# Recurrent stage in a written order: VectorE and ScalarE as listed, one conversion moved to GpSimd, weights earlier

## The chip, the cores and the metric

The kernel runs on one core of one Trainium2 chip. The metric is the device time of the whole kernel in microseconds, as the median of several runs. One execution was also recorded by the hardware profiler; its own time stands beside its trace. Engines: PE (TensorE, matrix products), DVE (VectorE), ACT (ScalarE), POOL (GpSimd), SP (SyncE, which issues most DMAs).

## The reference, cut to what matters

Two decoder layers on 1024 positions of width 1024 in fp32. Layer 0 is causal attention with 12 heads (low-rank queries and keys, rotary parts); layer 1 is a gated linear recurrence. Both layers also attend with 4 heads to 256 memory tokens, multiply by a SiLU gate, project out and normalise.

```python
def causal_attention(q, k, v):                      # layer 0, 12 heads
    sc = einsum('bqhd,bkhd->bhqk', q_blk, k) * scale
    p = softmax(where(mask, sc, -inf))
    return einsum('bhqk,bkhd->bqhd', p, v)

def rg_lru_branch(u, ...):                          # layer 1
    xc = conv_b + sum(u_pad[:, t:t + s] * conv_w[t] for t in range(4))
    xb = xc.reshape(b, s, 12, 64)
    r = sigmoid(einsum('bsgi,gij->bsgj', xb, w_r) + b_r)
    i = sigmoid(einsum('bsgi,gij->bsgj', xb, w_i) + b_i)
    log_a = (-8 * softplus(-lam)) * r
    a = exp(log_a)
    gated_x = sqrt(-expm1(2 * log_a)) * (i * xc)
    return scan(h = a * h + gated_x)

for layer in range(2):
    z = h @ w_in                                    # mixer inputs | gate | q_mem
    tok = causal_attention(...) if layer == 0 else rg_lru_branch(...)
    mem_out = memory_attention(q_mem, mem_k, mem_v)
    y = concat([tok, mem_out]) * silu(gate)
    h = layer_norm(ALPHA * h + y @ w_out)
```

## The kernel before

**Split numbers.** A product of two fp32 matrices is made of three products on PE with operands split into a high part (rounded to the format PE reads fast) and a low part (the rest). `split` (lines 88 to 90) makes both: the high part by the engine named, always the low part by DVE (line 90). `load_w` (line 98) loads a block of weights of 128 x 1024 into one of two staging tiles `wf` by a DMA on SP's queue and splits it into the next pair of a ring of tiles, with the high part by GpSimd in this stage (line 82).

**The recurrent stage** (lines 939 to 1082) works on six tiles t of 128 channels by 1024 positions. For each tile:

- u: 48 products of 512 columns (`proj_T`, lines 113 to 115) project the layer's input by the weights `w1[t]` into a pair of PSUM banks. u0 and u1 come first, while layer 0's last norm blocks still finish; their weights are in tiles `st`, those of later ones in R16/R17 or rg0/rg1 by turns.
- c (`lru_copy`): ACT copies the two banks to U.
- v (`lru_conv`): DVE makes the convolution, one two-operand step (line 1006) and three three-operand ones (line 1009) in place in XC, which read U and XC, both in SBUF. XC is then split into XH and XL; XH is made by ACT here.
- r (`lru_rest`): 12 gate products of XH and XL on PE into two pairs of banks, four sigmoids on ACT into RR and II; then on ACT an exponential (a), a hyperbolic tangent, the square of a (written over XC, line 1027) and a square root (line 1029), and on DVE the product II*XC (line 1026), a combination of XC and RR (line 1028), the product RR*II (line 1030) and the scan (line 1031).

U, XC, XH, XL, RR and II have two buffers, chosen by t mod 2. After the six tiles follow two projections for the memory queries (q0, q1; `qmem_proj`) and gate blocks 6 and 7 (g).

**Who sets the order.** Each engine runs its own instructions strictly in order. The program is written in the order of the string `ORD`, and a scheduler of the build rearranges all engines by its own estimates; a section under `tc.manual_schedule(engines=...)` keeps the named engines in the order in which the program is written. Before, no engine was kept in this stage. What each engine then has is quoted in the section on the change.

**Two other places.** In layer 0, `max_pass` finds each query's largest score for a coming head while the current heads are worked on. `neg_max_row` then waits `DELAY` units of work (3; a unit is one block of scores) and has PE transpose the maxima (line 433); DVE copies them (line 435), and a DMA puts them into a row of the query tile. After each pair of heads, `finish_pair` (line 624) sends the denominators through memory and multiplies the pair by their reciprocals on GpSimd (line 634). Slots 0 to 5 are the pairs of layer 0's heads, 6 and 7 the memory heads of layer 0, 8 and 9 those of layer 1. In `attn_unit` the low part of the softmax weights (`pl`, in layer 1 `mpl`, line 564) comes from DVE or GpSimd, and PE's products wait for it.

Of the kernel before, what the change touches and what calls it, by code (L numbers as in the profile page):

```python
# [15 lines left out]
ALU = mybir.AluOpType  # L16
# [4 lines left out]
S = 1024  # L21
# [23 lines left out]
def hybrid_kernel(ctx: ExitStack, tc: tile.TileContext, io):  # L45
    nc = tc.nc
    PE, ACT, DVE, POOL, SP = nc.tensor, nc.scalar, nc.vector, nc.gpsimd, nc.sync
# [6 lines left out]
    def open_pool(name, side="left"):  # L54
        p = tc.tile_pool(name=name, bufs=1, reuse_waits="tile", side=side)
        return p, p.__enter__()
# [8 lines left out]
    R16 = main.tile([128, S], F32R, name="R16")  # L65
    R17 = main.tile([128, S], F32R, name="R17")
# [21 lines left out]
    def split(src, hi, lo, eng):  # L88
        hi_copy(eng, hi, src)
        DVE.tensor_tensor(out=lo, in0=src, in1=f32(hi), op=ALU.subtract)  # L90

    wjob = [0]
    ring = {"hi": [R[10], R16], "lo": [R[11], R17]}
# [6 lines left out]
    def load_w(ap, n):  # L100
        j = wjob[0]
        wjob[0] += 1
        st = wf[j % 2][:, :n]
        SP.dma_start(st, ap)
        nb = len(ring["hi"])
        hi, lo = ring["hi"][j % nb], ring["lo"][j % nb]
        wsplit(st, hi[:, :n], lo[:, :n])
        return hi, lo
# [143 lines left out]

    HALF = [slice(0, 512), slice(512, 1024)]

    def qmem_proj(layer, m, ap, mh, ml, thi, tlo, ps):
        hi, lo = load_w(ap, S)
        proj_T(ps, hi, lo, mh, ml, 8)
        for n, cs in enumerate(HALF):
            ACT.copy(thi[n], ps[n])
            DVE.tensor_tensor(out=tlo[n], in0=ps[n], in1=f32(thi[n]), op=ALU.subtract)  # L260
            SP.dma_start(qmem_d[layer][m, 0][:, cs], f32(thi[n]))
            SP.dma_start(qmem_d[layer][m, 1][:, cs], f32(tlo[n]))

    for m in range(2):
        qmem_proj(0, m, io["w0"][8 + m], lambda n: [x[:, HALF[n]] for x in xh], lambda n: [x[:, HALF[n]] for x in xl],
                  ph[2 * m:2 * m + 2], pl[2 * m:2 * m + 2], next_ps())


# [109 lines left out]
    def run_all(g):  # L378
        for _ in g:
            pass  # L380
# [43 lines left out]
                rows.remove(r)  # L424
                r[1]()

    def neg_max_row(mx, dst_row):
        nm = small.tile([128, 8], F32, tag="nm", name="nm")
        DVE.tensor_reduce(out=nm, in_=mx, axis=AX.X, op=ALU.max, negate=True)

        def row():
            ps = next_m()
            PE.transpose(ps[0:8, 0:128], nm, ident)
            nmt = small.tile([8, 128], F32R, tag="nmt", name="nmt", bufs=1)
            DVE.tensor_copy(nmt, ps[0:8, 0:128])
            SP.dma_start(f32(dst_row()).rearrange("o (a b) -> o a b", a=8), f32(nmt))
        rows.append([DELAY, row])

    def max_pass(h, halves=None):
        kh_, kl_, qh_, ql_ = sets[h % 4] if not halves else [None] * 4  # L440
        mx = small.tile([128, 8, 2], F32, tag="mx", name="mx")
        POOL.memset(mx, -3.0e38)
        for i in range(8):
            n = (i + 1) * 128
            step = 320 if n == 640 and not halves else 512
            for a in range(0, n, step):
                w = min(step, n - a)
                j = min(a, 512) // step
                out = next_m()[:, 0:w]
                if halves:  # L450
                    q, k = halves[2 + i // 4][0:96, i % 4 * 128:(i % 4 + 1) * 128], halves[a // 512][0:96, 0:w]
                else:
                    q, k = qh_[0:96, i * 128:(i + 1) * 128], kh_[0:96, a:a + w]
                PE.matmul(out, q, k, start=True, stop=True)  # L454
                if a + w == (i + 1) * 128:
                    DVE.tensor_tensor_reduce(out=out, in0=out, in1=cmask[:, 512 - w:512], scale=1.0, scalar=-3.0e38,  # L456
                                             op0=ALU.add, op1=ALU.max, accum_out=mx[:, i, j:j + 1])
                else:
                    DVE.tensor_reduce(out=mx[:, i, j:j + 1], in_=out, axis=AX.X, op=ALU.max)
                yield  # L460
        neg_max_row(mx, lambda: sets[h % 4][2][96:97, :])
        yield

    sets = [[p0[1].tile([128, S], F32R, tag=f"g{j}", name=f"st0_{j}") for j in range(4)]]
# [159 lines left out]
    def finish_pair(gt, slot):  # L624
        rn = small.tile([128, 16], F32, tag="rn", name="rn")
        for e in range(2):
            SP.dma_start(rn[:, e * 8:(e + 1) * 8], den[32 * e:32 * e + 1, :].rearrange("o (a b) -> o a b", a=128))
        DVE.reciprocal(rn, rn)
        for e in range(2):
            SP.dma_start(den_d[slot, e].rearrange("(a b) -> a b", a=128), rn[:, e * 8:(e + 1) * 8])  # L630
        rec = Of[slot % 2]
        for e in range(2):
            SP.dma_start(rec[e * 64:(e + 1) * 64, :], den_d[slot, e:e + 1, :].broadcast_to([64, S]))
        POOL.tensor_tensor(out=gt, in0=gt, in1=rec, op=ALU.mult)

    SC = 1.0 / math.sqrt(96.0)

# [305 lines left out]

    weng[0] = POOL
    wjob[0] = 0
    ring["hi"], ring["lo"] = [sets[i][2] for i in (1, 2, 3)], [sets[i][3] for i in (1, 2, 3)]
    u_ps = []
    for t in range(2):
        hi, lo = load_w(io["w1"][t], S)
        ps = pair(t)  # L950
        proj_T(ps, hi, lo, hth, htl, 8)
        u_ps.append(ps)
# [3 lines left out]
    G1 = GA + [pc0[1].tile([128, S], F32, name=f"GB{i}") for i in range(4)]  # L956
    rg = [pc0[1].tile([128, S], F32R, name=f"rg{i}") for i in range(2)]
    ring["hi"], ring["lo"] = [R16, rg[0]], [R17, rg[1]]
    pc = open_pool("pc")
    U = [pc[1].tile([128, S + 3], F32, name=f"U{i}") for i in range(2)]  # L960
    XC = [pc[1].tile([128, S], F32, name=f"XC{i}") for i in range(2)]
# [37 lines left out]
    def lru_copy(t, ps):  # L999
        for n in range(2):  # L1000
            ACT.copy(U[t % 2][:, 3 + n * 512:3 + (n + 1) * 512], ps[n])

    def lru_conv(t):
        b = t % 2
        up, xc = U[b], XC[b]
        DVE.tensor_scalar(out=xc, in0=up[:, 0:S], scalar1=vecs[:, CW + 4 * t:CW + 4 * t + 1],
                          scalar2=vecs[:, CB + t:CB + t + 1], op0=ALU.mult, op1=ALU.add)
        for j in range(1, 4):
            DVE.scalar_tensor_tensor(out=xc, in0=up[:, j:j + S], scalar=vecs[:, CW + 4 * t + j:CW + 4 * t + j + 1],
                                     in1=xc, op0=ALU.mult, op1=ALU.add)  # L1010
        split(xc, XH[b], XL[b], ACT)

    def lru_rest(t):
        b = t % 2
        xc, rr, ii = XC[b], RR[b], II[b]
        for w, (dst, bias) in enumerate(((rr, BR), (ii, BI))):
            ps = pair(3 * (1 - w))
            o = t * 256 + w * 128
            proj_T(ps, WGH[:, o:o + 128], WGL[:, o:o + 128], lambda n: [XH[b][:, HALF[n]]],
                   lambda n: [XL[b][:, HALF[n]]], 1)  # L1020
            for n, cs in enumerate(HALF):
                ACT.activation(dst[:, cs], ps[n], AF.Sigmoid, bias=vecs[:, bias + t:bias + t + 1])
        a = G1[t]
        ACT.activation(a, rr, AF.Exp, scale=cf[:, t:t + 1])
        ACT.activation(rr, rr, AF.Tanh, scale=cf[:, t:t + 1])
        DVE.tensor_tensor(out=ii, in0=ii, in1=xc, op=ALU.mult)
        ACT.activation(xc, a, AF.Square)
        DVE.scalar_tensor_tensor(out=rr, in0=xc, scalar=1.0, in1=rr, op0=ALU.add, op1=ALU.mult)
        ACT.activation(rr, rr, AF.Sqrt, scale=-1.0)
        DVE.tensor_tensor(out=ii, in0=rr, in1=ii, op=ALU.mult)  # L1030
        DVE.tensor_tensor_scan(out=G1[t], data0=a, data1=ii, initial=0.0, op0=ALU.mult, op1=ALU.add)
# [3 lines left out]
    def next_p():  # L1035
        psj[0] += 1
        return pair(1 + (psj[0] - 1) % 2)

    def lru_u(t):
        hi, lo = load_w(io["w1"][t], S)  # L1040
        ps = next_p()
        proj_T(ps, hi, lo, hth, htl, 8)
        u_ps.append(ps)

    gw = {}
    gorder = [6, 7, 0, 1, 2, 3, 4, 5]

    def gate_load(m):
        gw[m] = load_w(io["w1"][6 + m], S)
# [13 lines left out]
                DVE.tensor_tensor(out=G1[m][:, cs], in0=ps[n], in1=G1[m][:, cs], op=ALU.mult)  # L1063
            yield

    ORD = 'c0 v0 c1 v1 r0 u2 c2 v2 r1 u3 c3 v3 r2 u4 c4 v4 r3 u5 c5 v5 r4 q0 r5 q1 g6 g7'
    for it in ORD.split():
        t = int(it[1])
        if it[0] == 'c':
            lru_copy(t, u_ps[t])  # L1070
        elif it[0] == 'v':
            lru_conv(t)
        elif it[0] == 'r':
            lru_rest(t)
        elif it[0] == 'u':
            lru_u(t)
        elif it[0] == 'g':
            gate_load(t)
            run_all(gate1(t, next_p()))
        else:  # L1080
            qmem_proj(1, t, io["w1"][14 + t], hth, htl, [QH[:, c] for c in HALF], [QL[:, c] for c in HALF], next_p())
    close_pool(pc)

    pd = open_pool("pd")
# [120 lines left out]
```

## Time and profile before

| | |
|---|---|
| median of 3 runs | 928.58 us (928.46 to 929.18) |
| the profiled execution | 926.91 us, of which the span from first to last instruction is 925.1 us |
| PE busy | 896.5 us (97%) |
| DVE, ACT, POOL busy | 594.9, 442.5, 223.6 us |
| mean granted clock of PE | 0.994 of full speed |

Idle time counts where it is PE's, since PE is busy nearly all the time. A timeline row gives the start and the duration in us, the engine, the source line, the operation, what it writes and reads, and in brackets how long the engine stood idle before it and what ended that. Matrix products are pipelined: one of 512 columns is shown with 0.39 us, but the next starts some 0.233 us later.

### The profile page before, as it was taken

How to read it: one execution, taken by the hardware profiler on the slowest of the kernel's cores; microseconds unless marked ns; L12 is line 12 of the kernel's file. 1: busy time of each engine (PE TensorE's matmuls, PEld its weight loads, DVE VectorE, ACT ScalarE, POOL GpSimd, SP SyncE). 2: the span in 40 equal slices, each digit the busy share in tenths (PEclk: the TensorE clock that was granted, in tenths of full speed). 3: DMA queues.
4: the chain of work that ended last, by engine and by line, in shares of the span. 5: the costliest groups of instructions: out<-in, count | busy, mean ns of one | idle time of the engine just before them, and what ended most of it. 6: DMA issues, size and time to landing. Idle time of an engine off the chain costs nothing.

```text
span 925.1 us, 12456 instructions
## 1 busy us (share of the span) xinstructions
PE 896.5 (97%) x4477; PEld 734.5 (79%) x4477; DVE 594.9 (64%) x1207; ACT 442.5 (48%) x764; POOL 223.6 (24%) x219
## 2 busy tenths in 40 slices
PE   9999999999999999999999999988999999999996
PEld 8998888877787778779676888866888877678886
DVE  7953346258877768796785597636997154457655
ACT  4422311217676677776785222117997156753000
POOL 5100023111526364473682100000000032210000
PEclk9999999999999999999999999998999999999999
DMA  8102133314022213055647653111112911252411
GB/s 309 63 16 108 55 102 127 125 63 116 17 61 69 59 58 105 15 150 159 202 117 239 203 191 102 53 69 46 45 46 109 242 50 47 69 183 91 153 75 46
DMA packets 45945, 96.08 MB, mean 104 GB/s; under 512 B 10906, under 2 KB 20282, under 8 KB 45884
## 3 DMA queue, kind: packets, MB, share of 16 engines
q1 hardware_dynamic: 45308, 94.47, 32.7%
q8 instruction: 35, 0.57, 0.3%
q10 hardware_dynamic: 576, 0.82, 0.3%
q14 instruction: 26, 0.21, 0.1%
HBM read 71.94 MB, written 23.16 MB: 103 GB/s over the span
## 4 chain that ended last, share of the span: by engine, by line
PE 81%; DVE 7%; ACT 6%; issue 3%; DMA 2%; POOL 1%; SPq 0%; DVEq 0%; ACTq 0%; POOLq 0%
PE bank L113 10%; PE bank L114 10%; PE bank L115 10%; PE bank L846 6%; PE bank L847 6%; PE bank L848 6%; PE bank L572 6%; PE bank L657 5%; PE bank L367 3%; PE bank L369 3%; PE bank L368 3%; PE bank L154 2%; PE bank L155 2%; PE bank L153 2%; PE bank L454 2%
## 5 line engine op out<-in xcount | busy, mean ns | idle before, releaser
L564 POOL TENSOR_TENSOR pl<-Pf,ph 128x512 fp32r<-128x512 f32 (+1 forms) x99 | 125.5, 1277 | 115.5 <-ACT ph L562 102.4
L561 ACT ACTIVATE Pf<-bank 128x512 f32<-128x512 f32 (+1 forms) x152 | 86.4, 569 | 50.2 <-DVE bank L558 20.0
L657 PE MATMUL bank<-st,st 96*128 96x512 f32 (+7 forms) x432 | 105.4, 343 | 0.1
L90 DVE TENSOR_TENSOR R<-wf,R 128x1024 fp32r<-128x1024 f32 (+4 forms) x43 | 52.6, 1226 | 63.9 <-POOL R L82 59.9
L657 PEld LDWEIGHTS bank<-st,st 96*128 96x128 f32 (+1 forms) x432 | 75.5, 189 | 13.3 <-ACT ph L562 0.6
L562 ACT ACTIVATE ph<-bank 128x512 fp32r<-128x512 f32 (+1 forms) x136 | 76.3, 562 | 0.1
L82 POOL TENSOR_SCALAR R<-wf 128x1024 fp32r<-128x1024 f32 (+3 forms) x25 | 24.1, 966 | 199.3 <-PE bank L114 96.1
L113 PE MATMUL bank<-R,R 128*128 128x256 f32 (+1 forms) x190 | 63.2, 333 | 0.7 <-ACT Pf L375 0.4
L114 PE MATMUL bank<-R,R 128*128 128x256 f32 (+1 forms) x190 | 62.3, 328 | 0.0
L115 PE MATMUL bank<-R,R 128*128 128x256 f32 (+1 forms) x190 | 62.2, 327 | 0.0
L456 DVE CUSTOM_DVE_ANT_0 bank<-bank,cmask 128x384 f32<-128x384 f32 (+4 forms) x96 | 48.8, 518 | 9.8 <-PE bank L454 9.0
L367 PE MATMUL bank<-xh,R 128*128 128x512 f32 x128 | 50.9, 398 | 0.1
L369 PE MATMUL bank<-xh,R 128*128 128x512 f32 x128 | 50.7, 396 | 0.0
L368 PE MATMUL bank<-xl,R 128*128 128x512 f32 x128 | 50.5, 395 | 0.0
L572 PE MATMUL bank<-ph,VH 128*65 128x512 f32 (+2 forms) x144 | 49.3, 342 | 0.0
L123 ACT ACTIVATE rq_t<-lnv 128x1 f32<-128x1 f32 x16 | 3.3, 203 | 94.3 <-DVE lnv L897 94.3
L572 PE MATMUL bank<-pl,VH 128*65 128x512 f32 (+2 forms) x144 | 44.9, 339 | 2.3 <-POOL pl L564 1.9
L892 DVE SCALAR_TENSOR_TENSOR GA<-GA,bank 128x512 f32<-128x512 f32 (+1 forms) x34 | 22.0, 648 | 38.9 <-PE bank L848 38.6
L572 PE MATMUL bank<-ph,VL 128*65 128x512 f32 (+2 forms) x144 | 46.8, 337 | 0.0
L847 PE MATMUL bank<-wo,yh 128*128 128x512 f32 (+1 forms) x126 | 46.8, 372 | 0.0
L846 PE MATMUL bank<-wo,yh 128*128 128x512 f32 (+1 forms) x126 | 46.7, 370 | 0.0
L848 PE MATMUL bank<-wo,yl 128*128 128x512 f32 (+1 forms) x126 | 45.9, 368 | 0.0
(313 smaller groups left out, 2444.0 us busy)
## 6 DMA issues: line engine op xcount, KB each, us to landing
wf<-w SPq DMA_DIRECT2D x26, 512.0 KB, 3.5
wf<-wout SPq DMA_DIRECT2D x16, 512.0 KB, 4.2
Of<-den_d SPq DMA_DIRECT2D x20, 256.0 KB, 3.6
GA<-x SPq DMA_DIRECT2D x8, 512.0 KB, 3.9
h_d<-GA SPq DMA_DIRECT2D x8, 512.0 KB, 2.6
GA<-h_d SPq DMA_DIRECT2D x8, 512.0 KB, 4.0
y_d<-GA SPq DMA_DIRECT2D x7, 512.0 KB
out<-GA SPq DMA_DIRECT2D x7, 512.0 KB
```

Of the source, the lines that this page charges most:

```text
L113: PE.matmul(out, lh, rh, start=(i == 0), stop=False)
L114: PE.matmul(out, lh, rl, start=False, stop=False)
L115: PE.matmul(out, ll, rh, start=False, stop=(i == n - 1))
L367: PE.matmul(ps[n], hi[:, ks], xh[k][:, cs], start=(k == 0), stop=False)
L369: PE.matmul(ps[n], lo[:, ks], xh[k][:, cs], start=False, stop=(k == 7))
L561: ACT.activation(pf[:, :n], ps[:, :n], AF.Exp, scale=scale)
L564: lo_eng.tensor_tensor(out=lo[:, :n], in0=pf[:, :n], in1=f32(hi)[:, :n], op=ALU.subtract)
L572: mm.append(lambda: PE.matmul(ops[0:65, q0:q0 + w], st, mv[:, c0:c0 + w], start=start, stop=stop))
L657: yield lambda: PE.matmul(ps[:, c0:c0 + w], k[0:r, ks], q[0:r, qs], start=(i == 0), stop=(i == 2))
L846: PE.matmul(out, hi, woh[k][:, ns], start=(k == ko[0]), stop=False)
L847: PE.matmul(out, hi, wol[k][:, ns], start=False, stop=False)
L848: PE.matmul(out, lo, woh[k][:, ns], start=False, stop=(k == ko[7]))
```

## The change

Six things, all in the order of work or in who does it:

- In the recurrent stage DVE and ACT are kept in the written order, and `ORD` is written anew. `lru_rest` is cut in two: `lru_gates` (letter r) keeps the gate products and the sigmoids, and `lru_rest` (letter b) the remaining ACT and DVE work. The next tile's convolution (v) is listed behind the gates and ahead of the next b.
- XH is made by GpSimd, not by ACT.
- The weights are loaded two steps ahead (letters l, k, h), where before each load came with its use. Those of u2 and u3 are asked for before the projections of u0 and u1 are made, ahead of the gate matrices `wg` on SP's queue.
- u0 and u1 keep their weights in the `st` tiles 1 and 3, where they were in 1 and 2.
- `qmem_proj` takes weights that are loaded already.
- For even heads the maxima are transposed 5 units later, where it was 3.
- The product in `finish_pair` is made by DVE for slots 7, 8 and 9.

```diff
-    def qmem_proj(layer, m, ap, mh, ml, thi, tlo, ps):
-        hi, lo = load_w(ap, S)
+    def qmem_proj(layer, m, w, mh, ml, thi, tlo, ps):
+        hi, lo = w
...
-    def neg_max_row(mx, dst_row):
+    def neg_max_row(mx, dst_row, delay=DELAY):
...
-        rows.append([DELAY, row])
+        rows.append([delay, row])
...
-        neg_max_row(mx, lambda: sets[h % 4][2][96:97, :])
+        neg_max_row(mx, lambda: sets[h % 4][2][96:97, :], 5 if h % 2 == 0 else DELAY)
...
-        POOL.tensor_tensor(out=gt, in0=gt, in1=rec, op=ALU.mult)
+        eng = DVE if slot >= 7 else POOL
+        eng.tensor_tensor(out=gt, in0=gt, in1=rec, op=ALU.mult)
...
-    ring["hi"], ring["lo"] = [sets[i][2] for i in (1, 2, 3)], [sets[i][3] for i in (1, 2, 3)]
+    ring["hi"], ring["lo"] = [sets[i][2] for i in (1, 3)], [sets[i][3] for i in (1, 3)]
     u_ps = []
+    uw = [load_w(io["w1"][t], S) for t in range(2)]
+    ring["hi"], ring["lo"] = [R16], [R17]
+    gw = {2: load_w(io["w1"][2], S)}
     for t in range(2):
-        hi, lo = load_w(io["w1"][t], S)
+        hi, lo = uw[t]
...
     ring["hi"], ring["lo"] = [R16, rg[0]], [R17, rg[1]]
+    gw[3] = load_w(io["w1"][3], S)
...
-        split(xc, XH[b], XL[b], ACT)
-
-    def lru_rest(t):
+        split(xc, XH[b], XL[b], POOL)
+
+    def lru_gates(t):
         b = t % 2
         xc, rr, ii = XC[b], RR[b], II[b]
         for w, (dst, bias) in enumerate(((rr, BR), (ii, BI))):
...
                 ACT.activation(dst[:, cs], ps[n], AF.Sigmoid, bias=vecs[:, bias + t:bias + t + 1])
+
+    def lru_rest(t):
+        b = t % 2
+        xc, rr, ii = XC[b], RR[b], II[b]
         a = G1[t]
...
     def lru_u(t):
-        hi, lo = load_w(io["w1"][t], S)
+        hi, lo = gw[t]
...
-    ORD = 'c0 v0 c1 v1 r0 u2 c2 v2 r1 u3 c3 v3 r2 u4 c4 v4 r3 u5 c5 v5 r4 q0 r5 q1 g6 g7'
+    ORD = ('c0 v0 c1 r0 u2 v1 b0 c2 v2 l4 r1 u3 b1 c3 v3 l5 r2 u4 b2 c4 v4 k0 r3 u5 b3 c5 v5 k1 '
+           'r4 b4 q0 h6 r5 b5 q1 h7 g6 g7')
+    with tc.manual_schedule(engines={mybir.EngineType.DVE, mybir.EngineType.Activation}):
+        for it in ORD.split():
...
+            elif it[0] == 'b':
+                lru_rest(t)
+            elif it[0] == 'l':
+                gw[t] = load_w(io["w1"][t], S)
+            elif it[0] == 'k':
+                gw[t + 20] = load_w(io["w1"][14 + t], S)
...
+            elif it[0] == 'h':
+                gate_load(t)
```

VectorE at the start of the stage, where tiles 0 and 1 are convolved: what stood there before.

```order
L1006 TENSOR_SCALAR XC0_5392<-U0_5390,vecs_69 128x1024
L1006 TENSOR_SCALAR XC1_5393<-U1_5391,vecs_69 128x1024
L1009 SCALAR_TENSOR_TENSOR XC0_5392<-U0_5390,vecs_69,XC0_5392 128x1024
L1009 SCALAR_TENSOR_TENSOR XC1_5393<-U1_5391,vecs_69,XC1_5393 128x1024
L1009 SCALAR_TENSOR_TENSOR XC0_5392<-U0_5390,vecs_69,XC0_5392 128x1024
```

And what stands there now (WGL is the low part of the gate matrices):

```order
L1011 TENSOR_SCALAR XC0_5398<-U0_5396,vecs_69 128x1024
L1014 SCALAR_TENSOR_TENSOR XC0_5398<-U0_5396,vecs_69,XC0_5398 128x1024 x2
L90 TENSOR_TENSOR WGL_5411<-wf1_83,WGH_5410 128x768
L1014 SCALAR_TENSOR_TENSOR XC0_5398<-U0_5396,vecs_69,XC0_5398 128x1024
L90 TENSOR_TENSOR XL0_5402<-XC0_5398,XH0_5400 128x1024
L1011 TENSOR_SCALAR XC1_5399<-U1_5397,vecs_69 128x1024
```

Tile 0's convolution and split are now complete before tile 1's first step; before, the two tiles took turns.

VectorE in the loop, from the recurrence of tile 0 to that of tile 1, before (R17 is the low part of a weight block, GA0 the scan's result):

```order
L1026 TENSOR_TENSOR II0_5400<-II0_5400,XC0_5392 128x1024
L1028 SCALAR_TENSOR_TENSOR RR0_5398<-XC0_5392,RR0_5398 128x1024
L1030 TENSOR_TENSOR II0_5400<-RR0_5398,II0_5400 128x1024
L1006 TENSOR_SCALAR XC0_5392<-U0_5390,vecs_69 128x1024
L1031 SCALAR_TENSOR_TENSOR GA0_72<-GA0_72,II0_5400 128x1024
L1009 SCALAR_TENSOR_TENSOR XC0_5392<-U0_5390,vecs_69,XC0_5392 128x1024
L1026 TENSOR_TENSOR II1_5401<-II1_5401,XC1_5393 128x1024
L1009 SCALAR_TENSOR_TENSOR XC0_5392<-U0_5390,vecs_69,XC0_5392 128x1024
L90 TENSOR_TENSOR R17_71<-wf0_82,R16_70 128x1024
L1009 SCALAR_TENSOR_TENSOR XC0_5392<-U0_5390,vecs_69,XC0_5392 128x1024
L1028 SCALAR_TENSOR_TENSOR RR1_5399<-XC1_5393,RR1_5399 128x1024
L90 TENSOR_TENSOR XL0_5396<-XC0_5392,XH0_5394 128x1024
```

And now:

```order
L1035 TENSOR_TENSOR II0_5406<-II0_5406,XC0_5398 128x1024
L1037 SCALAR_TENSOR_TENSOR RR0_5404<-XC0_5398,RR0_5404 128x1024
L1039 TENSOR_TENSOR II0_5406<-RR0_5404,II0_5406 128x1024
L1040 SCALAR_TENSOR_TENSOR GA0_72<-GA0_72,II0_5406 128x1024
L1011 TENSOR_SCALAR XC0_5398<-U0_5396,vecs_69 128x1024
L1014 SCALAR_TENSOR_TENSOR XC0_5398<-U0_5396,vecs_69,XC0_5398 128x1024 x3
L90 TENSOR_TENSOR XL0_5402<-XC0_5398,XH0_5400 128x1024
L90 TENSOR_TENSOR R17_71<-wf0_82,R16_70 128x1024
L1035 TENSOR_TENSOR II1_5407<-II1_5407,XC1_5399 128x1024
```

The product II1*XC1 stood in the middle of the next convolution; it now stands behind that convolution, its split and a weight's low part.

GpSimd in the same stretch (XH of tiles 0 to 3; R16 and rg0 are high parts of weight blocks) has, with nothing but weight splits there before:

```order
L82 TENSOR_SCALAR XH0_5400<-XC0_5398 128x1024
L82 TENSOR_SCALAR R16_70<-wf0_82 128x1024
L82 TENSOR_SCALAR XH1_5401<-XC1_5399 128x1024
L82 TENSOR_SCALAR rg0_5388<-wf1_83 128x1024
L82 TENSOR_SCALAR XH0_5400<-XC0_5398 128x1024
```

One weight split comes before each conversion of XC from the second on.

## Rows read from the trace of the kernel before

**Rows 1.** The page, part 1: busy us (share of the span) xinstructions.

```profile
PE 896.5 (97%) x4477; PEld 734.5 (79%) x4477; DVE 594.9 (64%) x1207; ACT 442.5 (48%) x764; POOL 223.6 (24%) x219
```

**Rows 2.** What PE waited for: us in total, times, longest.

```profile
PE bank L113 <- ACT XH L84: 6.9, 1, 6.9
...
PE bank L572 <- DVE mpl L564: 1.5, 1, 1.5
...
PE bank L433 <- DVE mx L456: 1.3, 3, 0.5
```

**Rows 3.** Timeline of PE around the start of the recurrent stage.

```profile
619.66 0.39 PE L113 MATMUL bank<-HTh,R 128*128 128x512 f32 x1
...
628.53 2.08 PE L113 MATMUL bank<-XH,WGH 128*128 128x512 f32 x4 [6.86 <-ACT XH L84]
...
632.78 0.39 PE L115 MATMUL bank<-HTh,R 128*128 128x512 f32 x1
```

**Rows 4.** Windows: length, busy us (x) of PE, PEld, DVE, ACT, POOL, clock, DMA.

```profile
625.00:626.00 1.00, 0.00 (x0) 0.00 (x0) 1.00 (x1) 0.00 (x0) 0.00 (x0) 0.50 0.00 0
804.00:806.00 2.00, 1.27 (x6) 0.94 (x7) 1.96 (x3) 0.94 (x2) 0.13 (x1) 1.00 0.18 57
```

**Rows 5.** Timeline of PE: first gate products of two tiles, 60 products apart.

```profile
670.04 0.40 PE L113 MATMUL bank<-XH,WGH 128*128 128x512 f32 x1
...
684.03 0.39 PE L113 MATMUL bank<-XH,WGH 128*128 128x512 f32 x1
```

**Rows 6.** Timeline of DVE at the start of the recurrent stage.

```profile
620.55 0.81 DVE L1006 TENSOR_SCALAR XC<-U,vecs 128x1024 f32<-128x1024 f32 x1 [8.48 <-ACT U L1001]
621.28 7.26 DVE L1009 SCALAR_TENSOR_TENSOR XC<-U,vecs,XC 128x1024 f32<-128x1024 f32 x6
```

**Rows 7.** Timeline of POOL at three places.

```profile
479.77 2.40 POOL L634 TENSOR_TENSOR GA<-GA,Of 128x1024 f32<-128x1024 f32 x1 [1.67 <-DMA Of<-den_d]
...
656.11 1.05 POOL L82 TENSOR_SCALAR rg<-wf 128x1024 fp32r<-128x1024 f32 x1 [12.00 <-PE bank L114]
...
801.75 2.38 POOL L634 TENSOR_TENSOR GB<-GB,Of 128x1024 f32<-128x1024 f32 x1 [7.12 <-DMA Of<-den_d]
```

**Rows 8.** Timeline of DVE in the loop.

```profile
628.51 1.23 DVE L90 TENSOR_TENSOR XL<-XC,XH 128x1024 fp32r<-128x1024 f32 x1
629.65 1.22 DVE L90 TENSOR_TENSOR R<-wf,R 128x1024 fp32r<-128x1024 f32 x1
...
680.87 1.23 DVE L1028 SCALAR_TENSOR_TENSOR RR<-XC,RR 128x1024 f32<-128x1024 f32 x1
...
684.91 1.26 DVE L1030 TENSOR_TENSOR II<-RR,II 128x1024 f32<-128x1024 f32 x1 [1.63 <-ACT RR L1029]
686.20 2.29 DVE L1031 TENSOR_TENSOR_SCAN GA<-GA,II 128x1024 f32<-128x1024 f32 x1
688.41 0.79 DVE L1006 TENSOR_SCALAR XC<-U,vecs 128x1024 f32<-128x1024 f32 x1
...
692.58 2.60 DVE L1009 SCALAR_TENSOR_TENSOR XC<-U,vecs,XC 128x1024 f32<-128x1024 f32 x2
```

**Rows 9.** Timeline of ACT in the loop.

```profile
631.50 1.27 ACT L1022 ACTIVATE RR<-bank,vecs 128x512 f32<-128x512 f32 x2 [0.57 <-PE bank L115]
...
637.47 1.04 ACT L1027 ACTIVATE XC<-GA 128x1024 f32<-128x1024 f32 x1
...
679.77 1.06 ACT L1027 ACTIVATE XC<-GA 128x1024 f32<-128x1024 f32 x1 [1.45 <-DVE II L1026]
...
683.82 1.06 ACT L1029 ACTIVATE RR<-RR 128x1024 f32<-128x1024 f32 x1
```

**Rows 10.** Timeline of DVE beside the first and the last row of group 7.

```profile
479.89 3.37 DVE L90 TENSOR_TENSOR R<-wf,R 128x1024 fp32r<-128x1024 f32 x1
...
802.35 2.93 DVE L564 TENSOR_TENSOR mpl<-Pf,mph 128x512 fp32r<-128x512 f32 x2 [1.79 <-ACT mph L562]
```

**Rows 11.** Timeline of PE in the memory attention of layer 1.

```profile
804.73 0.45 PE L572 MATMUL bank<-mpl,VH 128*65 128x512 f32 x1 [1.52 <-DVE mpl L564]
```

More of the change, by code (lines that the diff above doesn't have):

```diff
@@ L264, in hybrid_kernel @@
     for m in range(2):
-        qmem_proj(0, m, io["w0"][8 + m], lambda n: [x[:, HALF[n]] for x in xh], lambda n: [x[:, HALF[n]] for x in xl],
+        qmem_proj(0, m, load_w(io["w0"][8 + m], S), lambda n: [x[:, HALF[n]] for x in xh], lambda n: [x[:, HALF[n]] for x in xl],
                   ph[2 * m:2 * m + 2], pl[2 * m:2 * m + 2], next_ps())
@@ L1043, in lru_u @@
         u_ps.append(ps)
-    gw = {}
     gorder = [6, 7, 0, 1, 2, 3, 4, 5]
@@ L1064, in gate1 @@
             yield
-    ORD = 'c0 v0 c1 v1 r0 u2 c2 v2 r1 u3 c3 v3 r2 u4 c4 v4 r3 u5 c5 v5 r4 q0 r5 q1 g6 g7'
[L1067 to L1081, printed above, removed]
+    ORD = ('c0 v0 c1 r0 u2 v1 b0 c2 v2 l4 r1 u3 b1 c3 v3 l5 r2 u4 b2 c4 v4 k0 r3 u5 b3 c5 v5 k1 '
+           'r4 b4 q0 h6 r5 b5 q1 h7 g6 g7')
+    with tc.manual_schedule(engines={mybir.EngineType.DVE, mybir.EngineType.Activation}):
+        for it in ORD.split():
+            t = int(it[1])
+            if it[0] == 'c':
+                lru_copy(t, u_ps[t])
+            elif it[0] == 'v':
+                lru_conv(t)
+            elif it[0] == 'r':
+                lru_gates(t)
+            elif it[0] == 'b':
[4 more added lines that the diff above has]
+                gw[t + 20] = load_w(io["w1"][14 + t], S)
+            elif it[0] == 'u':
+                lru_u(t)
+                del gw[t]
+            elif it[0] == 'h':
+                gate_load(t)
+            elif it[0] == 'g':
+                run_all(gate1(t, next_p()))
+            else:
+                qmem_proj(1, t, gw.pop(t + 20), hth, htl, [QH[:, c] for c in HALF], [QL[:, c] for c in HALF], next_p())
     close_pool(pc)
```

## The prediction

> **What bounds the kernel now.** I read the page first: TensorE (PE) is busy 896.5 of 925.1 us [rows 1], so almost any microsecond must come out of, or go into, the places where PE stands still. The list of what PE waits for names them [rows 2]. The largest is one wait of 6.9 us for the product-ready tile XH at the start of the recurrent stage; three waits for the maxima transpose (L433) add 1.3 us, and one wait for `mpl` 1.5 us. All three are touched by the change. Elsewhere PE hardly waits, so edits there cost or gain next to nothing unless they make a new wait.
>
> Then the timelines. PE starts on the second pair of weights at 619.66 and runs dry; at 628.53 it goes on after 6.86 us idle [rows 3]. The granted clock fell during the idle time (0.50 in the slice from 625, the lower of its two levels, [rows 4]), and the products behind it are slow: the 12 gate products from 628.53 to 632.78 took 4.25 us, where 12 steps of the usual 0.233 us (60 products from 670.04 to 684.03, [rows 5]) are 2.80. That is 1.45 us more, so the stall costs 8.3 us. Its cause is on VectorE [rows 6]: tile 1's first convolution step stood ahead of the rest of tile 0's chain and waited 8.48 us for U until 620.55 (tile 0's first step was over by 612.1), and the six remaining steps ran in turns behind it.
>
> **The change, part by part.** *Start.* VectorE now finishes tile 0 alone and PE gets 42 products of the third u-projection ahead of gate r0: 619.66 + 42 x 0.233 = 629.5. Tile 0's convolution goes on from 612.1 (perhaps 1.2 us later, since u0 ends five products later) and needs some 8 us with its split by the links below, so XH and XL are ready 8 us early. The extra weight split (1.2 us) slides into the layer norm of block 7, whose transposes the new order puts five products (1.2 us) later. Gain 8.3 us, none lost there. Gate r1 follows 30 products after r0, at 636.5. GpSimd can convert XH1 only behind the weights of u4, which need the end of u2 (633.6): 633.6 + 1.05 + 1.05 + latencies = 635.8, so 0.7 us of cover is left, and XL1 keeps as much.
>
> *The loop.* This is where the order decides. Before, the steps of a later tile's convolution lie between the four recurrence operations, and VectorE has work while ScalarE computes a square or a root. Now VectorE does one tile's recurrence, then the next convolution, then waits for GpSimd, all in a row, and ScalarE's square overwrites XC, so it waits for the product II*XC. One round, link by link, each from its row: first step 0.82 and three dependent steps of 1.30 (0.79 at 688.41; two in 2.60 at 692.58), 4.7 us; GpSimd's conversion 1.05 [rows 7] with 0.1 of latency, 1.15; XL and the weights' low part 1.14 each (628.51 to 629.65), 2.3; II*XC 1.26 with latency; square 1.05 and RR 1.27 (680.87 follows the square begun at 679.77 by 1.10), 2.35; root 1.09; product and scan 1.26 and 2.21 (684.91, 686.20, 688.41) [rows 8, 9]. Sum 16.3 us. PE needs 14.0 us for the same round [rows 5].
>
> GpSimd also splits a weight per round (1.05 us, [rows 7]) as soon as PE has left the old one. That is 12.2 us after XL (8 + 44 products, [rows 5]), in the middle of the convolution, whose steps read two SBUF tiles. At 479.89 a VectorE subtraction of two SBUF tiles took 3.37 instead of 1.23 us [rows 8, 10] beside a 2.40 us GpSimd product begun 0.12 us earlier [rows 7]. I take the whole 1.0 us a round: 17.3 us. The other end is nothing (16.3), and if consecutive steps cost the 1.20 of the interleaved six [rows 6], 16.0.
>
> The Trainium skill ("SBUF — State Buffer", section "Who interferes with whom") says that a VectorE instruction with two SBUF inputs and a GpSimd instruction that reads SBUF exclude each other for a whole instruction. The row at 479.89 agrees (3.37 us), though no row here shows the convolution step itself beside GpSimd. By the rule the round is 17.3 us, without it 16.3.
>
> Gates r2 to r5 pay. For r2: r0's first bank is done 8 products after 629.5, at 631.5; in the new order the table load itself waits for that, so 1.3 us go before the sigmoids; the square is 5.97 us behind the first sigmoid (631.50 to 637.47, [rows 9]), at 638.8. From there 2.35 + 1.09 + 1.26 + 2.21 + 4.7 + 1.0 + 1.15 give XH2 at 652.6. PE reaches r2 82 products after r0, at 648.6: it waits 4.0, and 0.3 more for XL. r3, r4 and r5 each come 17.3 - 14.0 = 3.3 us late. Sum 4.3 + 9.9 = 14.2 us; with the low ends 3.0 + 3 x 2.0 = 9.0, and with 3.6 a round and a stretch at the lower clock behind the last wait (1.45, as above) 4.6 + 10.8 + 1.5 = 16.9.
>
> After r5 PE has 44 products of q1 and the last two gates' weights (48 each) before it needs anything new; VectorE's weight parts are ready 1 to 2 us before their use by the same sums, and SyncE's loads for memory attention are issued some 17 us ahead of their use, so nothing follows there.
>
> *Weights two steps ahead.* The loads move up on SP's queue, past the gate-matrix load (wg). That load moves behind two stores, and the second part is wanted only between two steps of tile 0's convolution, which has 8 us to spare. Nothing, covered by the u-projections.
>
> *ScalarE* loses six conversions (1.05 each). It is not the limit of the round: its own work ends some 4 us before the product that the square waits for. Nothing.
>
> *Maxima rows two units later.* The transpose no longer comes just after its reduction: 1.3 us [rows 2]. The row is then some three units ahead of its use. Bounds 0 to 1.5.
>
> *Last pairs' products.* The product on GpSimd (2.38 us from 801.75) held both `mpl` subtractions on VectorE (2.93 us for two, 802.35) [rows 7, 10], and PE waited 1.52 us [rows 11]. On VectorE it comes between the two and costs 1.23. The first `mpl` is on time, the second late by little: gain 1.5, bounds 0 to 1.7. For the earlier slot 7 no wait stands behind it.
>
> *Sum.* -8.3 - 1.3 - 1.5 + 14.2 = +3.1 us. The profiled execution took 926.91, so 930.0; the median of the timed runs is 1.67 higher, 928.58, so 931.7 for them.
>
> **The rivals.** *A, the round is shorter.* GpSimd's weight split finds a gap on VectorE, and steps follow as closely as in [rows 6]. r2 costs 3.0 to 3.3 and the others 2.0 to 2.3: 9.0 to 10.2, less 11.1, is -2.1 to -0.9: about 927. For it: no row shows exactly this pair of instructions together. Against: the 3.37 us.
>
> *B, faster: PE stays the limit of the loop.* Place: XH at gates r2 to r5. VectorE's busy time in a round is only about 12.6 us (the links above without the waits for ScalarE and GpSimd), and in the profile PE waits for nothing after r0. If the round hides its waits as before, the whole 11.1 us stay: 917.5. It decides when the round is under 16.0 us: there the loss drops under 9.2 and the change is faster by more than 0.2%; at 14.0 nothing is lost. Against it: the operations are serial by their data and the engine runs in the order given, and each link has a row.
>
> *C, the clock falls as well.* The 6.86 us wait brought the clock down; a wait of 1.52 us left it at 1.00 [rows 4, 11]. The new waits lie between the two. Slow products between two gates are absorbed by the next wait, so only the one after r5 counts, 1.5 us, and another if a wait behind it appears: 933.2 to 934.7. For: r2's wait is 4.0. Against: r5's is 3.0 at most in one piece, nearer to the short wait.
>
> **How the numbers follow.** My forecast (round of about 17.3, clock kept after r5) 0.48, between 929.8 and 933 by itself; A 0.22; B 0.12; C 0.18. About 0.2%, 1.9 us, is what a measurement of this kernel can tell. Faster than 926.7: B and a third of A, 0.20. Slower than 930.4: most of the forecast (0.39) and C (0.18), 0.57. Same: 0.23. The range that leaves out B and the upper end of C: 924.8 to 935.
>
> **What would show it.** Right: PE goes from 619.66 through u2 without a pause; its list of waits shows GpSimd's XH (four waits of 2.5 to 4 us) and the ones for L433 and `mpl` near 802 gone; gates r3 to r5 are about 17 us apart instead of 14; convolution steps beside a GpSimd weight split are about 1 us longer. Wrong in the loop: gates 14 us apart, no wait for XH (B), or 16 (A). Wrong at the start: a wait for XH at r0 or XH1 at r1. I should be most wrong if VectorE's links are not serial as I read them.

## The result and the profile after

The changed kernel takes 932.66 us (median of 20 runs) against 927.96 us of the kernel before in the same series: 4.7 us more. The ratio of the two sets of runs is 1.0059, 95% interval 1.0045 to 1.0072, so 5.5 us slower (4.2 to 6.7), which is also what their means differ by. The forecast was 931.7 for a kernel before of 928.58, 3.1 us slower. The profiled execution has a span of 932.5 us where before had 925.1. Part 1 of its page [rows 1]:

```profile
PE 903.1 (97%) x4477; PEld 737.3 (79%) x4477; DVE 597.3 (64%) x1210; ACT 436.2 (47%) x758; POOL 224.1 (24%) x222
```

PE has the same products as before and is busy 6.6 us longer: for the most part products ran at the lower clock, as the windows below show. What PE waited for [rows 2]:

```profile
PE bank L113 <- POOL XH L82: 8.6, 4, 3.7
PE bank L572 <- POOL pl L564: 2.6, 4, 1.4
...
PE bank L747 <- DVE mx L749: 1.0, 2, 0.6
...
PE bank L113 <- POOL R L82: 0.6, 1, 0.6
```

The one wait of 6.9 us for XH is gone, and four others for XH stand in its place. The lines for `mpl` and for the maxima transpose (L433) are gone too. PE's timeline shows the four: the first products of gates r2 to r5 [rows 3, 5], with idle time and releaser in brackets.

```profile
654.31 2.07 PE L113 MATMUL bank<-XH,WGH 128*128 128x512 f32 x4 [3.70 <-POOL XH L82]
...
671.99 1.19 PE L113 MATMUL bank<-XH,WGH 128*128 128x512 f32 x4 [1.09 <-POOL XH L82]
...
689.16 1.19 PE L113 MATMUL bank<-XH,WGH 128*128 128x512 f32 x4 [2.55 <-POOL XH L82]
...
706.39 1.21 PE L113 MATMUL bank<-XH,WGH 128*128 128x512 f32 x4 [1.22 <-POOL XH L82]
```

The gates are 17.68, 17.17 and 17.23 us apart; PE's 60 products need 13.99. So r3, r4 and r5 come 3.7, 3.2 and 3.2 us late. r2 stands 15.97 us behind r1 (638.34), with 52 products or 12.13 us between them: 3.8 late. Together 13.9 us. Not all of it is idle time: four products at 654.31 took 2.07 us, at 671.99 only 1.19. The windows (length, busy us of PE, PEld, DVE, ACT, POOL, then the granted clock) show why [rows 4]:

```profile
654.00:656.00 2.00, 1.69 (x4) 1.40 (x5) 1.71 (x2) 0.00 (x0) 0.25 (x1) 0.50 0.00 0
...
660.00:662.00 2.00, 2.00 (x10) 1.61 (x9) 0.85 (x2) 1.99 (x4) 0.00 (x0) 1.00 0.00 0
690.00:692.00 2.00, 1.93 (x6) 1.29 (x5) 2.00 (x3) 0.00 (x0) 0.00 (x0) 0.56 0.00 0
...
707.00:709.00 2.00, 1.95 (x9) 1.29 (x8) 2.00 (x3) 0.00 (x0) 0.00 (x0) 1.00 0.00 0
```

Behind the waits of 3.70 and 2.55 us the clock was at or near its lower level (0.50 and 0.56), behind that of 2.55 only after the first four products, which took 1.19 us as at 671.99; behind that of 1.22 it stayed at 1.00. What the slow products lost came out of the next wait, which is therefore short (1.09 and 1.22). A list of waits alone, 8.6 us, understates what this loop costs by 5 us. It also leaves out a short wait for XL at r3, r4 and r5: behind the four XH products of 671.99 the next product, the first to read XL, starts at 673.25, some 0.3 us later than without a pause and just behind the end of XL (671.97 and 1.23 us, below).

One round on VectorE, from one XL to the next, with the convolution steps before it [rows 8]:

```profile
665.63 3.92 DVE L1014 SCALAR_TENSOR_TENSOR XC<-U,vecs,XC 128x1024 f32<-128x1024 f32 x3
671.97 1.23 DVE L90 TENSOR_TENSOR XL<-XC,XH 128x1024 fp32r<-128x1024 f32 x1 [2.41 <-POOL XH L82]
673.11 1.22 DVE L90 TENSOR_TENSOR rg<-wf,rg 128x1024 fp32r<-128x1024 f32 x1
674.25 1.22 DVE L1035 TENSOR_TENSOR II<-II,XC 128x1024 f32<-128x1024 f32 x1
676.65 1.23 DVE L1037 SCALAR_TENSOR_TENSOR RR<-XC,RR 128x1024 f32<-128x1024 f32 x1 [1.19 <-ACT XC L1036]
679.03 1.23 DVE L1039 TENSOR_TENSOR II<-RR,II 128x1024 f32<-128x1024 f32 x1 [1.15 <-ACT RR L1038]
680.29 2.29 DVE L1040 TENSOR_TENSOR_SCAN GA<-GA,II 128x1024 f32<-128x1024 f32 x1
682.50 0.79 DVE L1011 TENSOR_SCALAR XC<-U,vecs 128x1024 f32<-128x1024 f32 x1
683.32 4.58 DVE L1014 SCALAR_TENSOR_TENSOR XC<-U,vecs,XC 128x1024 f32<-128x1024 f32 x3
689.14 1.23 DVE L90 TENSOR_TENSOR XL<-XC,XH 128x1024 fp32r<-128x1024 f32 x1 [1.24 <-POOL XH L82]
```

VectorE has no work beside any of its three waits: for ScalarE's square, for its root, for GpSimd's XH. The three convolution steps take 3.92 us in one round and 4.58 in the next. GpSimd's timeline [rows 7] tells the two kinds of round apart:

```profile
669.88 1.05 POOL L82 TENSOR_SCALAR R<-wf 128x1024 fp32r<-128x1024 f32 x1 [15.62 <-PE bank L114]
670.89 1.05 POOL L82 TENSOR_SCALAR XH<-XC 128x1024 fp32r<-128x1024 f32 x1
685.60 1.24 POOL L82 TENSOR_SCALAR rg<-wf 128x1024 fp32r<-128x1024 f32 x1 [13.66 <-PE bank L114]
688.06 1.05 POOL L82 TENSOR_SCALAR XH<-XC 128x1024 fp32r<-128x1024 f32 x1 [1.23 <-DVE XC L1014]
```

At 685.60 the weight split falls into the convolution and makes it 0.66 us longer. At 669.88 the slow products had delayed it past the convolution's end (at 669.55); it then stood in GpSimd's queue directly ahead of XH, which began 1.34 us after the convolution's end and not 0.16 as at 688.06: 1.2 us lost.

The product of the last pair, now on VectorE between two low parts, and PE behind it [rows 10, 11]:

```profile
811.53 0.69 DVE L564 TENSOR_TENSOR mpl<-Pf,mph 128x512 fp32r<-128x512 f32 x1 [1.79 <-ACT mph L562]
812.14 1.22 DVE L635 TENSOR_TENSOR GB<-GB,Of 128x1024 f32<-128x1024 f32 x1
813.28 0.68 DVE L564 TENSOR_TENSOR mpl<-Pf,mph 128x512 fp32r<-128x512 f32 x1
```

```profile
812.28 0.45 PE L572 MATMUL bank<-mpl,VH 128*65 128x512 f32 x1
```

The wait of 1.52 us is gone.

### The profile page after: what moved, and what is told of

Read it like the earlier page. It is cut to its first block, busy times and chain, and to the rows that moved or that the text cites. A ratio compares the mean times of both kernels' runs of the same rounds, so it can differ in the third digit from the quotient of the medians.

```text
span 932.5 us, 12480 instructions
## 1 busy us (share of the span) xinstructions
PE 903.1 (97%) x4477; PEld 737.3 (79%) x4477; DVE 597.3 (64%) x1210; ACT 436.2 (47%) x758; POOL 224.1 (24%) x222
## 4 chain that ended last, share of the span: by engine, by line
PE 83%; DVE 8%; ACT 4%; DMA 2%; POOL 1%; issue 1%; SPq 0%; DVEq 0%; ACTq 0%; POOLq 0%
PE bank L114 9%; PE bank L115 9%; PE bank L113 9%; PE bank L572 8%; PE bank L848 6%; PE bank L847 6%; PE bank L849 6%; PE bank L658 6%; PE bank L367 3%; PE bank L369 3%; PE bank L368 3%; PE bank L454 3%; PE bank L154 2%; PE bank L155 2%; PE bank L153 2%; DVE st L403 2%
## 5 line engine op out<-in xcount | busy, mean ns | idle before, releaser
L90 DVE TENSOR_TENSOR R<-wf,R 128x1024 fp32r<-128x1024 f32 (+4 forms) x43 | 49.8, 1162 | 58.0 <-POOL R L82 53.3
```

## Experiments

The ratios are to the kernel before in the same series of runs, with 95% intervals; times in us are medians. The changed kernel, timed once more beside the experiment on ScalarE's queue, stood at 1.0049 (1.0029 to 1.0070).

**One link less in the round.**

```diff
-    v2 l4 r1 u3 b1          # XL, low part of weights, II*XC, (square), combination ...
+    v2 r1 u3 a1 l4 y1 e1 s1 # b1 in four pieces: XL, II*XC, low part of weights, (square), combination ...
```

> The changed kernel with one link taken out of VectorE's serial round: the low part of the coming weights (1.22 us) is listed between II*XC and the combination that waits for ScalarE's square, where VectorE stands idle for 1.18 us, instead of ahead of II*XC. If the gates are set by VectorE's serial round (now 17.2 to 17.7 us), each of the gates r3, r4, r5 comes 1.1 us less late: rounds of about 16.1 to 16.5 us and 3 to 4 us less in all, some 929 us. If the round is set by something else (GpSimd's order, PE's own clock after a wait), the order on VectorE inside the round changes nothing and it stays at about 932.7.

Measured 929.35 us, ratio 1.0016 (0.9995 to 1.0038). GpSimd's timeline, three XH and a weight split:

```profile
670.54 1.04 POOL L82 TENSOR_SCALAR XH<-XC 128x1024 fp32r<-128x1024 f32 x1
685.65 1.05 POOL L82 TENSOR_SCALAR rg<-wf 128x1024 fp32r<-128x1024 f32 x1 [14.07 <-PE bank L114]
686.66 1.04 POOL L82 TENSOR_SCALAR XH<-XC 128x1024 fp32r<-128x1024 f32 x1
...
702.76 1.03 POOL L82 TENSOR_SCALAR XH<-XC 128x1024 fp32r<-128x1024 f32 x1
```

These rounds are 16.1 us, 1.1 less than 17.2; the one before them, from r2 to r3, is 17.05 for 17.68. So the order inside VectorE's round moves the gates. But VectorE's chain is no longer all that sets them: the convolution (3.93 us from 681.83) ends at 685.76, and XH begins only at 686.66. Ahead of it on GpSimd stands the weight split of 685.65 (1.05 us), which had to wait until PE had left the old weight, 14.0 us behind r3 (671.64). From a gate to the split, then XH, then the next gate is 14.0 + 1.05 + 1.04 = 16.1 us: as long as the split stands ahead of XH, no order on VectorE would make the round shorter (worked out from these rows, not tried). By its own links VectorE would have been ready some 0.7 us sooner.

**GpSimd without the weights.**

```diff
+    weng[0] = ACT          # high parts of the weights of l, k, h by ScalarE
     with tc.manual_schedule(...):
```

> The changed kernel with the high parts of the loop's weights made by ScalarE, so that GpSimd has nothing in the loop but XH. Theory: the weight split costs a round either 0.66 us (beside the convolution, which it holds up) or 1.24 us (in GpSimd's queue just ahead of XH); without it the rounds are 16.4 to 16.5 us, all four gates together 3.5 us earlier, about 929 us, and every convolution's three later steps take 3.92 us. Rival: GpSimd's split is hidden and the convolution's 4.6 us are chance; then rounds stay at 17.2 us and the time at 932.7.

Measured 928.52 us, ratio 1.0010 (0.9986 to 1.0034). The profiled execution took 934.19 us; against the kernel before it lost 3.7 us between 500 and 550 us, ahead of this stage, and its rounds are read here.

```profile
672.49 1.06 POOL L82 TENSOR_SCALAR XH<-XC 128x1024 fp32r<-128x1024 f32 x1 [15.49 <-DVE XC L1014]
689.05 1.05 POOL L82 TENSOR_SCALAR XH<-XC 128x1024 fp32r<-128x1024 f32 x1 [15.50 <-DVE XC L1014]
705.58 1.05 POOL L82 TENSOR_SCALAR XH<-XC 128x1024 fp32r<-128x1024 f32 x1 [15.49 <-DVE XC L1014]
```

The rounds are 16.5 us (the gates 16.4 to 16.7 apart), and every convolution's three steps take 3.92 or 3.93. So the links of the sum make 16.5 us (forecast 16.3), and GpSimd's weight split makes the rest.

**The start alone.**

```diff
-    with tc.manual_schedule(engines={DVE, Activation}):   # the whole of ORD
+    # kept for c0 v0 c1 r0 u2 v1 alone; the rest of ORD to the scheduler
```

> The changed kernel with only the start (c0 v0 c1 r0 u2 v1) kept in the written order and the loop behind it left to the build's scheduler, which puts the first convolution step and the low part of the weights into VectorE's waits. Theory: the start keeps its gain of 8.3 us and the loop hides its waits as the kernel before did; 928 - 8 - 1.5 (mpl) = about 918 to 920. Rival: GpSimd's conversion alone makes the round too long for PE, whatever VectorE's order; then waits for XH stay at r3 to r5 and it is 925 or more.

Measured 920.27 us, ratio 0.9936 (0.9909 to 0.9963). One wait for XH is left, at r2:

```profile
PE bank L113 <- POOL XH L82: 2.4, 1, 2.4
```

That wait, which the expectation did not have, puts the time at its upper end. From r2 on the gates are 13.5 to 14.0 us apart, with XH by GpSimd all the same. The written order of the loop is what costs; the start keeps its gain. Two orders differ here, though, VectorE's and GpSimd's: from r3 on GpSimd makes XH (660.25) ahead of the weight split (665.27) and not behind it. What either is worth by itself was not tried.

**A woven order.**

```diff
-    c2 v2 l4 r1 u3 b1 c3 v3 ...
+    u3 c3 r1 a1 l5 y1 v3 e1 x3 s1 ...   # PE and GpSimd kept in this order too
+    # a: II*XC  l: low part of weights (ScalarE squares)  y: combination
+    # v: convolution (ScalarE's root)  e: product (GpSimd's XH)  x: XL  s: scan
```

> The changed kernel with an order written so that no wait of VectorE is empty: II*XC, low part of the weights (while ScalarE squares), combination, the next convolution (while ScalarE takes the root), product (while GpSimd converts XH), XL, scan; PE and GpSimd kept in the written order too, each gate a whole u-projection behind its XH. VectorE then needs about 13.1 us a round by the rows of the loop, less than PE's 14.0, so PE should wait for nothing from u0 to g7: the 14 us of waits go and 917 us is expected (916 to 920). Rival: contention between VectorE and GpSimd or a wait that I have not seen keeps the round above 14 us: gates more than 14.2 us apart, and above 922 us.

Measured 916.73 us, ratio 0.9881 (0.9851 to 0.9911): 11 us faster than before by the ratio, the best kernel here. PE waits for no XH, and its gates are 13.95 or 13.99 us apart. VectorE's round is 14.69 us, not 13.1, because product and XH, and XL and the weight split, now run side by side. XH also stands ahead of the weight split on GpSimd here. VectorE and GpSimd:

```profile
659.34 1.22 DVE L1047 TENSOR_TENSOR II<-RR,II 128x1024 f32<-128x1024 f32 x1
661.51 2.05 DVE L1020 TENSOR_TENSOR XL<-XC,XH 128x1024 fp32r<-128x1024 f32 x1 [0.94 <-POOL XH L82]
```

```profile
659.61 1.86 POOL L82 TENSOR_SCALAR XH<-XC 128x1024 fp32r<-128x1024 f32 x1 [11.80 <-PE bank L115]
661.44 1.05 POOL L82 TENSOR_SCALAR R<-wf 128x1024 fp32r<-128x1024 f32 x1
```

XH takes 1.86 instead of 1.05 us, so that VectorE waits 0.94 us for it, and XL takes 2.05 instead of 1.23. XH is nevertheless early: that of r2 is ready at 646.8 and wanted at 657.4, a lead that shrinks by 0.7 us a round. By that trend PE would still not wait with two more tiles, and would with some ten more (an estimate; not tried).

**XH back on ScalarE.**

```diff
-        split(xc, XH[b], XL[b], POOL)
+        split(xc, XH[b], XL[b], ACT)
```

> The changed kernel with XH made by ScalarE as before, GpSimd keeping only the weight splits. Theory: the order on VectorE is what lengthens the round, and GpSimd's part is only the 0.7 to 1.2 us that its weight split adds; with XH off its queue the split can no longer stand ahead of XH, and may only hold up the convolution where it falls on it: rounds of 16.4 to 17.2 us, waits for XH (now by ScalarE) still before r2 to r5, about 929 to 931 us. Rival: the hand-over of XH to GpSimd is the cause; then with ScalarE the waits go and it is near 918.

Measured 947.11 us, ratio 1.0212 (1.0191 to 1.0234). Neither expectation held. PE's waits and ScalarE's timeline:

```profile
PE bank L113 <- ACT RR L1027: 19.6, 4, 6.5
```

```profile
672.27 1.04 ACT L84 CAST XH<-XC 128x1024 fp32r<-128x1024 f32 x1 [7.98 <-DVE XC L1014]
673.33 1.28 ACT L1027 ACT_TABLE_LOAD   x1
674.62 1.26 ACT L1027 ACTIVATE RR<-bank,vecs 128x512 f32<-128x512 f32 x2
675.78 1.27 ACT L1027 ACTIVATE II<-bank,vecs 128x512 f32<-128x512 f32 x2
```

In the written order the next tile's XH stands ahead of this tile's sigmoids on ScalarE: v1 is listed behind the gates r0, but v2 to v5 ahead of r1 to r4 (the section on the change has v behind the gates throughout). XH waits 7.98 us for the convolution, and table load, sigmoids, exponential and tangent wait behind it; the gates are 20.0 to 20.7 us apart. I had counted the instruction and not what is queued behind it.

**XH on ScalarE behind the tangent.**

```diff
-    c2 v2 l4 r1 u3 b1       # ScalarE: XH2, sigmoids 1, exp 1, tanh 1, square 1
+    c2 r1 p1 v2 l4 u3 b1    # ScalarE: sigmoids 1, exp 1, tanh 1, XH2, square 1
```

> The kernel with XH by ScalarE again, but with the current tile's sigmoids, exponential and tangent listed ahead of the next tile's XH on ScalarE; VectorE's order is that of the changed kernel. If it was ScalarE's queue (XH ahead of the sigmoids) that made the rounds 20 to 20.7 us, they fall to 16.4 to 17.2 us, PE's waits name XH again and not the sigmoids, and it takes 928 to 931 us. If ScalarE's XH is slow for another reason, the rounds stay near 20 us and the time near 945.

Measured 934.95 us, ratio 1.0063 (1.0040 to 1.0085). The rounds fall to 16.6 and 17.0 us and PE waits for XH again, so ScalarE's queue was the cause. The time is above the 928 to 931 expected: by the same order the first XH1 stands behind tile 0's tangent, XL1 ends at 641.2 (in the changed kernel at 638.9, where u0 began 1.8 us later), and PE waits 7.09 us before r2.

**The product alone.**

```diff
-        POOL.tensor_tensor(out=gt, in0=gt, in1=rec, op=ALU.mult)
+        eng = DVE if slot >= 7 else POOL
+        eng.tensor_tensor(out=gt, in0=gt, in1=rec, op=ALU.mult)
```

> The kernel before with one edit, the product of slots 7 to 9 by VectorE. The wait of 1.5 us for mpl near 803 goes and nothing takes its place: 1.5 us off (926 for 927.5). Rival: VectorE, now with 1.2 us more work there, is late for another mpl or for the memory attention's maxima, and the gain comes back within 30 us.

Measured 926.51 us, ratio 0.9984 (0.9967 to 1.0000). The wait is gone from the list. Product for product, PE is 3.1 us behind the profile of before at 800 us and 1.5 behind it at 806, past the place: 1.6 us come from there. In the changed kernel the same place gives 1.6 us (9.2 behind, then 7.6). The interval of the times alone reaches 1.0000.

**The maxima rows alone.**

```diff
-        neg_max_row(mx, lambda: sets[h % 4][2][96:97, :])
+        neg_max_row(mx, lambda: sets[h % 4][2][96:97, :], 5 if h % 2 == 0 else DELAY)
```

> The kernel before with one edit, the maxima of even heads transposed five units after instead of three. By the prediction the three waits for L433 (1.3 us) go and 1.3 us are gained. Rival, from the trace of the changed kernel: the time that PE no longer waits there is waited for GpSimd's low parts of the softmax weights (pl, 1.9 us before, 2.6 after), and half of it or less is left: 0 to 0.7 us.

Measured 927.92 us, ratio 1.0005 (0.9991 to 1.0019). The line for L433 is gone, and in its place the list of waits has:

```profile
PE bank L572 <- POOL pl L564: 2.5, 4, 1.4
...
PE bank L657 <- DMA st<-nmt: 0.7, 1, 0.7
```

GpSimd's `pl` took 1.9 us of PE's time before and now 2.5; the row itself, later by two units, is once not there when the next head wants it (0.7 us). Nothing is left of 1.3. The longer wait for `pl` comes with the later rows: near 410 us it is 0.7 us in the three profiles with rows at three units, and 1.4 in the nine others.

**The woven order with the rows as before.**

> The woven order with the maxima rows at three units as before, all else as in the woven kernel. If the later rows are worth 1.3 us, this takes 918; if their waits only change names, it stays within 0.7 us of the woven kernel's 916.7, and the wait for pl in layer 0 falls back from 2.6 to about 1.9 us while the one for L433 comes back.

Measured 917.49 us, ratio 0.9895 (0.9876 to 0.9914), not to be told from the woven kernel's 0.9881. `pl` costs 2.0 us and L433 1.3 again, as the second expectation said.

**The changed kernel again.**

> The changed kernel as it is, for its time beside the others and for a second profile. If the granted clock's fall behind the 1.30 us wait near 229.6 is chance (it came in 4 of 10 profiles with the same wait), a second profile may lack it and then ends some 1.5 us earlier; the loop's rounds stay at 17.2 to 17.7 us either way, since they follow from the order.

Measured 932.51 us. The second profile has the clock at 1.00 near 231 to 235 and a span of 929.2, 3.3 us less than the first: 1.5 by the clock, and 2.1 that lay between the two after 22 us already, ahead of everything that the change touches, less 0.3 that it lost behind that. Its waits before r2 to r5 are 3.69, 1.11, 2.58 and 1.11 us, and the gates are 18.1, 17.2 and 17.3 us apart, the first more than the 17.7 expected.

## Why the prediction was right

- *Start, -8.3 us.* Right. PE waits nowhere between 606 and 650 us, and r0 stands at 631.36, where 629.5 was forecast, 1.9 us of which the kernel was late on entry. The experiment on the start alone keeps it. That VectorE's order did it is not shown by itself: tile 0's XL is over at 621.59, and PE passes the old place of r0 at 623.46, so that order would do; but r0 also stands 34 products (7.9 us) further back in PE's list than before, more than the old wait of 6.86.
- *Gates r2 to r5, +14.2 us.* Right in sum and in the way: 3.8, 3.7, 3.2 and 3.2, together 13.9, for 4.3 and three of 3.3. The links make 16.5 us a round without the weight split (forecast 16.3). What I did not see is a second ring, from PE's old weight over the split to XH and the next gate, which by itself would keep the gates 16.1 us apart (the experiment with one link less).
- *GpSimd's weight split, 1.0 us a round.* Right in size (0.7 to 1.2), half right in kind. I placed every split in the middle of the convolution. Where it fell there it cost 0.66 us; where PE's slow products had put it off, it cost up to 1.2 in GpSimd's queue. By the rule of the Trainium skill ("SBUF — State Buffer", section "SBUF: two separate sides") a VectorE instruction with two SBUF inputs and a GpSimd instruction that reads SBUF exclude each other for a whole instruction; the traces agree in that each of the two is the longer one at some place (convolution 4.58 for 3.92 here, XH 1.86 for 1.05 in the woven order), though the convolution lost less than the split's 1.05 us.
- *Rival A* (16.0 to 16.3 a round) is near what is left without the weights on GpSimd: 16.5 us and 928.52 were measured there, about 927 forecast. *Rival B* needed rounds under 14.0 and is refuted for this order; the woven order shows that it was open to another one: VectorE's operations are serial only as far as they are listed so.
- *Rival C.* The clock fell, behind 3.70 and 2.55 us, but after r5 (1.22) it stayed at 1.00, so the slow products were absorbed by later waits as the forecast said.
- *Last pairs' product, -1.5 us.* Right: 1.6 us in the trace, 0.9984 in time.
- *Maxima rows, -1.3 us.* Wrong: 0, the lower bound. PE's next input was late by as much.
- *"Nothing follows" after r5.* Wrong by 1.7 us: product for product, PE is 7.5 us behind the kernel before at r5 and 9.2 at 765. Of that, 0.5 comes right behind r5, where PE also waits for XL; 0.8 at 731.7, where it waits 0.55 us for a weight block; and 0.4 around 764.2, where it waits 0.60 for the maxima of memory attention. For the weight block the trace shows that PE's list, which is not kept in the written order, now has a product with the next block (R, at 732.24) among the first of the present one (rg, from 731.06), while GpSimd splits R only from 731.14 on; before, the 48 products with rg came first. No run tried either place.
- *Weights two steps ahead, nothing.* Not tried alone. PE waits for no weight block from 606 us to r5.
- *ScalarE's conversions, nothing.* Right as busy time, but the reason was incomplete: with XH left on ScalarE, the same order takes 947 us.

With what was measured for each the sum is -8.3 - 1.6 + 13.9 + 1.7 = +5.7 us; product for product the trace has 5.5 (7.4 behind at the end, 1.9 on entry to the stage), and the timed runs 4.7 by medians and 5.5 by means, for a forecast of 3.1. The two terms that failed, the maxima rows and the time after r5, both went the slower way. That 931.7 comes within 1 us of 932.66 is in part luck: the three runs that the forecast started from had a median of 928.58, the series had 927.96. The span of the profiled execution is 7.4 us longer than that of before, 1.5 of it because its clock fell once more near 232, which is told at the end.

## What to carry to other kernels

An engine that is busy two thirds of the time can still set the pace when its list puts dependent operations in a row: add the round trips to other engines to the durations, and compare that sum with the bounding engine's round. Look for other rings too, such as a buffer that the bounding engine must leave before a helper's queue goes on. The remedy is the list, with independent work laid into each round trip: the same repair of the start ended 5.5 us slower with one set of lists for the loop and 11 us faster with another. A wait that vanishes from the bounding engine's list counts as a gain only if its next input is early; and an instruction moved in a queue is priced by what stands behind it.

## What was not expected of the hardware

The clock's fall behind a short wait is not certain. Near 230 us PE waits 1.3 us for VectorE's `st` in every profile taken; in the changed kernel's first profile the clock then fell, in that of the kernel before it did not:

```profile
231.00:236.00 5.00, 4.81 (x16) 3.52 (x17) 3.80 (x13) 2.42 (x6) 1.28 (x1) 0.69 0.17 56
```

```profile
231.00:236.00 5.00, 4.95 (x24) 3.60 (x24) 4.97 (x14) 2.78 (x6) 2.43 (x2) 1.00 0.10 40
```

It fell in 4 of 12 profiles, and cost 1.5 us each time (product for product, the changed kernel went from 0.6 to 2.1 us behind). A single profile can thus be 1.5 us off for a reason that lies in neither kernel.
